# A two-layer decoder trunk: gate projections moved from three earlier chunks to the last attention, with their input kept in DRAM

## The chip, the cores and the metric

The kernel runs on one core of one Trainium2 chip. The metric is the device time of one execution in microseconds (us). The engines are PE (TensorE, matmuls and transposes; its weight loads are counted as PEld), DVE (VectorE), ACT (ScalarE), POOL (GpSimd) and SP (SyncE, which here only issues DMAs). ACT and POOL issue some DMAs as well. Each engine works through its own instructions in order.

## The reference

Two layers over 2048 positions of width 1024, in float32. Layer 0 is a gated short convolution; keys and values are then computed once; layer 1 is a stick-breaking attention of 8 heads of 64, with its own query and SiLU gate.

```python
def _short_conv_mixer(h, w_in, w_conv, w_out):
    b_gate, c_gate, xin, g = jnp.split(h @ w_in, 4, axis=-1)
    y = b_gate * _causal_depthwise_conv(c_gate * xin, w_conv)
    return (y * jax.nn.silu(g)) @ w_out
# attention, for one block of 128 queries and all keys before them:
    z = jnp.einsum("bhqd,bhkd->bhqk", qb, kf[:, :, :kl]) * scale
    log_one_minus = jnp.where(mask, jax.nn.log_sigmoid(-z), 0.0)
    rev = lax.cumsum(log_one_minus, axis=3, reverse=True)
    weights = jnp.exp(jnp.where(mask, z + rev, -jnp.inf))
    outs.append(jnp.einsum("bhqk,bhkd->bhqd", weights, vf[:, :, :kl]))
# the whole:
    x = x + _short_conv_mixer(_rmsnorm(x, norm_a), w_in_a, conv_a, w_out_a)
    k, v = jnp.split(_rmsnorm(x, norm_kv) @ w_kv, 2, axis=-1)
    q, g = jnp.split(_rmsnorm(x, norm_b) @ w_in_b, 2, axis=-1)
    o = attention(q, k, v)
    x = x + (o * jax.nn.silu(g)) @ w_out_b
    return _rmsnorm(x, norm_f)
```

The product of the factors 1 - sigmoid(z) over the keys between a key and its query is what the kernel computes as a running product, so that a weight is sigmoid(z) times that product.

## The kernel before

The positions run backwards and are cut into four chunks of 512 (c = 0 to 3). All activations are kept transposed, channels on the 128 partitions and the 512 positions of the chunk on the free axis. A matmul operand is split into a high and a low float32r part (`split`: ACT casts, DVE or POOL subtracts), and a product is made of three matmuls (high by high, high by low, low by high). A group of 8 input blocks is 24 matmuls of 128x128 by 128x512 (`mm3`); `LIN` is the planner's cost of one such group.

Per chunk the work is:

- `mixer_in`: for each of 8 channel blocks the four groups C, X, B, G and the convolution; the result goes to DRAM. Chunks 0 and 1 go together at the start, and there the weights are loaded raw, split once, and the split weights stored in DRAM (`split_w`; 32 for the mixer, 16 for the key/value and the query/gate weights in `fold_gains`, 8 for `w_out_a` in the first `proj_out`, 8 for `w_out_b` near the end). All later uses load the split form. A split weight lies in one of four buffers (tag `whl`), a raw one in one of two (`wraw`). The store is issued on SP's queue.
- `proj_out`: 8 groups, the residual, and the normalised input `xn` of the projections, split, in one of two large buffers (tag `act`, `kept[c]`).
- `proj_k`, `proj_q`, `proj_v`, `proj_g`: four groups each from `kept[c]`. The gate's result goes through a sigmoid (ACT, L441) and a product (DVE, L442) to `sg_d` in DRAM.
- `attention`: for each head and each chunk of keys up to its own, four blocks of 128 queries: `z` by two matmuls (L486, L487), the two sigmoids on ACT (L489 into `R`, L491 into `w`), on the diagonal chunk two masks on POOL (L495), the running product along the keys on DVE (L500), the product with `w` on DVE (L504). Then the weights are transposed (L512), split, and multiplied with the values (L521, L522). The last column of an `R` is the carry to the next chunk of keys; for that POOL copies it into the first column of the next `R` (L499), which the product at L504 reads. There are five `R` buffers.
- `gated`, `out_b`, `out_stat`, `out_norm`: the attention's result times the gate, the output projection, and the last norm. The last head and the output of the last chunk are handled by `out_b_last`.

The order across phases is written by `merge`: it draws from several generators in turn, always from the one whose spent share of its planned cost is smallest. `F0` to `F4` are the shares of a mixer or an attention that go into one phase before the rest goes into the next; `TP` is the planned cost of all projections of one chunk. Within this order, which acts as a priority, the framework's scheduler places the instructions on the engines by its own model of time. In the last phases the matmul groups of the fill are cut into sixes and tied to the attention's progress (`fine`, `anchors`). The fill of the last attention before is `proj_rest(3)`, then the output projections and norms of chunks 0, 1 and 2.

Of the kernel before, what the change touches and what calls it, by code (L numbers as in the profile page):

```python
# [23 lines left out]

F0, F1, F2, F3, F4 = 0.4, 0.5, 0.65, 0.4, 0.6
S2, S3, S4, S7 = 2.0, 0.5, 3.0, 2.0
# [19 lines left out]
def kernel(  # L46
# [48 lines left out]
    q_d = [[dram.tile([P, 2, CH], F32, name=f"q_d_{c}_{h}") for h in range(NH // 2)] for c in range(NCH)]  # L95
    v_d = [dram.tile([P, 4, NH, 2, 64], F32, name=f"v_d_{c}") for c in range(NCH)]
    sg_d = [[dram.tile([P, CH], F32, name=f"sg_d_{c}_{h}") for h in range(NH // 2)] for c in range(NCH)]
    og_d = [[dram.tile([P, CH], F32, name=f"og_d_{c}_{h}") for h in range(NH // 2)] for c in range(NCH)]
# [90 lines left out]
    def split_w(raw, key, nm, kt=KD, eng=nc.vector):  # L189

        wt = w_tile(nm, kt)
        split(wt[:, 0], wt[:, 1], raw, eng)
        split_d[key] = dram.tile([P, 2, kt, P], F32, name=f"sw_{nm}")
        nc.sync.dma_start(out=split_d[key], in_=wt.bitcast(F32))
        return wt
# [176 lines left out]
    def proj_out(c):  # L372
# [22 lines left out]
        for k in range(KD):  # L395
            t = x1[:, k, :]
            nc.vector.tensor_mul(t, t, pb)
            split(xn[:, 0, k, :], xn[:, 1, k, :], t, nc.gpsimd if k in XNL else nc.vector)
        kept[c] = xn
        yield YP[c] * 24 * MM  # L400
# [51 lines left out]
    def proj_rest(c):  # L452
        yield from proj_k(c, 1)
        yield from proj_q(c, 1)
        yield from proj_v(c, 1)
        yield from proj_v(c, 2)
        yield from proj_v(c, 3)
        for i in (2, 3):
            yield from proj_k(c, i)
            yield from proj_q(c, i)  # L460
        for i in range(4):
            yield from proj_g(c, i)


    def attention(c, h, ot):
# [8 lines left out]
        for kc in range(c, -1, -1):  # L474
# [7 lines left out]
            for qi in range(4):  # L482
# [9 lines left out]
                if diag:  # L492

                    for blk, fill in ((R[:, lo + 1:lo + 1 + P], 1.0), (w[:, lo:lo + P], 0.0)):
                        nc.gpsimd.affine_select(out=blk, in_=blk, pattern=[[1, P]], base=0, channel_multiplier=-1,  # L495
                                                compare_op=ALU.is_gt, fill=fill)
                    nc.gpsimd.memset(R[:, lo:lo + 1], 1.0)
                else:
                    nc.gpsimd.tensor_copy(R[:, 0:1], carry[qi])  # L499
                nc.vector.tensor_tensor_scan(out=R[:, lo + 1:CH + 1], data0=R[:, lo + 1:CH + 1],  # L500
                                             data1=ones[:, 0:1].to_broadcast([P, CH - lo]),
                                             initial=R[:, lo:lo + 1] if diag else carry[qi], op0=ALU.mult, op1=ALU.mult)
                carry[qi] = R[:, CH:CH + 1]
# [168 lines left out]
    def chain(*gens):  # L672
        for g in gens:
            yield from g
# [23 lines left out]
    LIN = 24 * MM  # L698
    TA, TF, TR, TO = 32 * LIN, 11 * LIN, 13 * LIN, 4 * LIN

# [6 lines left out]
    def heads(lo, hi, c):  # L707
        for hb in range(lo, hi):
# [5 lines left out]
            else:  # L714
                nc.sync.dma_start(out=og_d[c][hb], in_=ot)

    TP = TF + TR
    m01 = mixer_in((0, 1))
# [12 lines left out]
    lo, hi = range(0, NB), range(NB, KD)  # L731
    fill = chain(proj_rest(3), gated_in(0), out_b(0, range(KD)), out_stat(0), gated_in(1),
                 out_b(1, lo), out_norm(0), out_b(1, hi), gated_in(2), out_stat(1),
                 out_b(2, lo), out_norm(1), out_b(2, hi), out_stat(2))
    merge((fill, TR + 3 * TO), (heads(0, 3, 3), 0.75 * ta(3)))
    tail = chain(gated_in(3, range(3)), take(last, NB * 9 * MM), out_norm(2), until(last, -1.0))
# [29 lines left out]
```

## Time and profile before

| | us |
|---|---|
| median of 3 runs | 1909.28 (1908.41 to 1910.37) |
| profiled execution | 1907.57 |
| span of its trace | 1905.8 |
| PE busy | 1784.0 |
| DVE busy | 1264.6 |
| ACT busy | 769.7 |
| POOL busy | 436.2 |

The span is from the first to the last instruction of the trace; the profiled execution is 1.8 us longer. A row of the profile such as `L442 DVE TENSOR_TENSOR sgb<-sgb,pg ... x16 | 10.9, 684 | 49.9 <-ACT sgb L441 49.9` reads: line 442 of the kernel, on DVE, writes `sgb` from `sgb` and `pg`, 16 times; 10.9 us busy in all and 684 ns for one; 49.9 us of idle time of its engine before them, most of which the named instruction ended. A row of the table by stretches gives the stretch and its length, then for each engine the busy us and the number of instructions, then the granted clock of PE, the busy share of the DMA engines and GB/s. A row of the waits gives who waited for whom, us in total, times, longest us. A row of the chain of waits gives the start, the length and the piece of work. A row of DMA issues ends in the size of one and the median us from issue to landing.

### The profile page before, as it was taken

Reading aid. Unit: us, or ns where it says so; the run is one execution under the profiler, and the core shown is the slowest. Engines: PE = TensorE matmul, PEld = TensorE weight load, DVE = VectorE, ACT = ScalarE, POOL = GpSimd, SP = SyncE. Lnnn points to the kernel's source line nnn. Section 1 sums busy time; section 2 is a strip of 40 time slices with the busy share of each in tenths; the row PEclk is TensorE's granted clock in tenths of the full one; section 3 lists DMA queues with packets and bytes.
Section 4 is the critical chain, followed back from the end, with each engine's and each line's share of the span. In section 5 each row is a group of like instructions: output and inputs, shape, how many; then the busy total and the mean of one; then the engine's idle time right before and its main releaser. Section 6 shows DMA issues by size and latency. Waiting matters only on the chain.

```text
span 1905.8 us, 24702 instructions
## 1 busy us (share of the span) xinstructions
PE 1784.0 (94%) x8312; PEld 1449.4 (76%) x8312; DVE 1264.6 (66%) x1895; ACT 769.7 (40%) x1481; POOL 436.2 (23%) x822
## 2 busy tenths in 40 slices
PE   7899999999999999999999999999979999878785
PEld 5787777778888888888788888888857788656563
DVE  7644554574334264428888346788897999999996
ACT  6312222241123133314545233444555666565553
POOL 5000000000011021103123112222422224654641
PEclk9999999999999999999999999999999999999897
DMA  9648787798887779776767776655746665877751
GB/s 314 210 150 248 248 254 237 243 312 304 295 284 270 258 237 286 246 262 224 242 211 268 238 253 219 202 175 197 258 144 196 197 199 193 284 225 250 252 177 50
DMA packets 226702, 443.64 MB, mean 233 GB/s; under 512 B 16912, under 2 KB 131600, under 8 KB 199952
## 3 DMA queue, kind: packets, MB, share of 16 engines
q1 hardware_dynamic: 166496, 383.30, 60.0%
q10 hardware_dynamic: 59920, 58.74, 10.9%
q8 instruction: 66, 1.08, 0.2%
q14 instruction: 60, 0.49, 0.1%
q0 software_dynamic: 160, 0.02, 0.1%
HBM read 314.34 MB, written 127.66 MB: 232 GB/s over the span
## 4 chain that ended last, share of the span: by engine, by line
PE 69%; DVE 14%; DMA 9%; issue 4%; ACT 2%; POOL 1%; SPq 0%; ACTq 0%; POOLq 0%; DVEq 0%
PE pX L216 8%; PE po L216 7%; PE pG L216 7%; PE pC L216 7%; PE pB L216 6%; PE pg L216 5%; PE pk L216 5%; PE pq L216 5%; PE pv L216 4%; PE wt L512 4%; DVE R L500 4%; PE av L522 3%; DVE w L504 2%; PE av L521 2%; PE z L486 2%
## 5 line engine op out<-in xcount | busy, mean ns | idle before, releaser
L500 DVE TENSOR_TENSOR_SCAN R<-R,R,ones 128x512 f32<-128x512 f32 x192 | 256.6, 1339 | 11.4 <-ACT R L489 11.1
L489 ACT ACTIVATE R<-z 128x512 f32<-128x512 f32 (+1 forms) x320 | 174.2, 544 | 173.1 <-DVE R L500 78.4
L174 DVE TENSOR_TENSOR wtl<-wt,wth 128x512 fp32r<-128x512 f32 (+1 forms) x320 | 185.6, 600 | 67.2 <-ACT wth L173 66.3
L504 DVE TENSOR_TENSOR w<-w,R 128x512 f32<-128x512 f32 (+1 forms) x320 | 212.2, 671 | 21.3 <-POOL R L499 3.0
L173 ACT CAST wth<-wt 128x512 fp32r<-128x512 f32 (+1 forms) x320 | 160.3, 526 | 160.1 <-PE wt L512 137.4
L216 PE MATMUL pC<-h,whl_C 128*128 128x512 f32 x768 | 197.1, 405 | 14.4 <-ACT whl_C L173 8.3
L216 PE MATMUL pG<-h,whl_G 128*128 128x512 f32 x768 | 186.6, 393 | 9.9 <-ACT whl_G L173 9.9
L499 POOL COPY R<-R 128x1 f32<-128x1 f32 x192 | 112.3, 585 | 360.8 <-DVE R L500 293.3
L216 PE MATMUL pX<-h,whl_X 128*128 128x512 f32 x768 | 187.6, 393 | 6.0 <-ACT cs L320 3.9
L216 PE MATMUL po<-y,whl_o 128*128 128x512 f32 x768 | 187.8, 394 | 2.0 <-DVE x L389 1.3
L512 PE MATMUL wt<-ident,w 128*128 128x128 f32 x1088 | 177.8, 278 | 9.2 <-DVE w L504 5.1
L216 PEld LDWEIGHTS pC<-h,whl_C 128*128 128x128 f32 x768 | 148.2, 195 | 49.4 <-ACT whl_C L173 8.3
L216 PE MATMUL pB<-h,whl_B 128*128 128x512 f32 x768 | 185.6, 392 | 0.0
L216 PEld LDWEIGHTS pG<-h,whl_G 128*128 128x128 f32 x768 | 143.2, 188 | 41.0 <-ACT whl_G L173 11.6
L491 ACT ACTIVATE w<-z 128x512 f32<-128x512 f32 (+1 forms) x320 | 172.7, 543 | 0.5 <-PE wt L512 0.5
L216 PEld LDWEIGHTS pX<-h,whl_X 128*128 128x128 f32 x768 | 142.2, 188 | 37.6 <-ACT cs L320 5.1
L216 PEld LDWEIGHTS po<-y,whl_o 128*128 128x128 f32 x768 | 144.2, 189 | 33.5 <-DVE x L389 1.9
L512 PEld LDWEIGHTS wt<-ident,w 128*128 128x128 f32 x1088 | 138.6, 143 | 38.3 <-DVE w L504 7.2
L216 PEld LDWEIGHTS pB<-h,whl_B 128*128 128x128 f32 x768 | 143.0, 188 | 30.1 <-DVE cv L356 0.4
L522 PE MATMUL av<-wtl,vv 128*128 128x512 f32 (+1 forms) x320 | 129.1, 405 | 36.7 <-DVE wtl L174 36.6
L500 DVE TENSOR_TENSOR_SCAN R<-R,ones 128x512 f32<-128x512 f32 (+3 forms) x128 | 116.1, 913 | 33.8 <-POOL R L495 32.2
L486 PE MATMUL z<-kt,q 128*128 128x512 f32 (+1 forms) x320 | 129.1, 405 | 4.1 <-ACT w L491 3.4
(170 smaller groups left out, 2655.3 us busy)
## 6 DMA issues: line engine op xcount, KB each, us to landing
whl_o<-sw_o SPq DMA_DIRECT2D x24, 1024.0 KB, 5.7
kt<-k_d ACTq DMA_DIRECT2D x80, 256.0 KB, 3.6
vv<-v_d ACTq DMA_DIRECT2D x80, 256.0 KB, 4.0
whl_C<-sw_C SPq DMA_DIRECT2D x16, 1024.0 KB, 5.4
whl_X<-sw_X SPq DMA_DIRECT2D x16, 1024.0 KB, 5.5
whl_B<-sw_B SPq DMA_DIRECT2D x16, 1024.0 KB, 5.5
whl_G<-sw_G SPq DMA_DIRECT2D x16, 1024.0 KB, 5.2
whl_k<-sw_kv SPq DMA_DIRECT2D x16, 1024.0 KB, 5.2
```

The lines of the kernel that those rows point to most:

```text
L173: nc.scalar.copy(hi, src)
L174: eng.tensor_sub(lo, src, hi.bitcast(F32))
L216: ins = nc.tensor.matmul(ps, w[:, k, :], a[:, m, k, :], start=n == 0, stop=n == 3 * kt - 1)
L486: nc.tensor.matmul(ps[:, lom:CH], q2[:, 0, qi * P:(qi + 1) * P], kt[:, lom:CH], start=True, stop=False)
L489: nc.scalar.activation(R[:, lo + 1:CH + 1], ps[:, lo:CH], AF.Sigmoid, scale=-0.125)
L491: nc.scalar.activation(w[:, lo:CH], ps[:, lo:CH], AF.Sigmoid, scale=0.125)
L499: nc.gpsimd.tensor_copy(R[:, 0:1], carry[qi])
L500: nc.vector.tensor_tensor_scan(out=R[:, lo + 1:CH + 1], data0=R[:, lo + 1:CH + 1], data1=ones[:, 0:1].to_broadcast([P, CH - lo]), initial= ...
L504: nc.vector.tensor_mul(w[:, lo:CH], w[:, lo:CH], R[:, lo:CH])
L512: nc.tensor.transpose(wt[:, qi * P:(qi + 1) * P], ws[qi][:, kb * P:(kb + 1) * P], ident)
L521: nc.tensor.matmul(av[:, 0:n], vs, wh[:, 0:n], start=first, stop=False)
L522: ins = nc.tensor.matmul(av[:, 0:n], vs, wl[:, 0:n], start=False, stop=final)
```

## The change

The normalised, split input `xn` of chunks 0, 1 and 2 is also stored in DRAM, piece by piece, on POOL's queue. The four gate groups of these chunks leave `proj_rest` and become `proj_gate`, which reloads `xn` into a buffer of the tag `act` on SP's queue; in the fill of the last attention they stand behind those of chunk 3 and ahead of the output projections. The planned costs and four of the five shares are changed to go with it. Two further edits come along: the store of every split weight is issued on POOL's queue in place of SP's, and in the attention the carry is no longer copied into `R`: the first column of `R` is set to 1 by a POOL memset, and the running product starts at that column with the carry as its initial value.

```diff
-F0, F1, F2, F3, F4 = 0.4, 0.5, 0.65, 0.4, 0.6
+F0, F1, F2, F3, F4 = 0.3, 0.25, 0.6, 0.35, 0.6
...
+    xn_d = [dram.tile([P, 2, KD, CH], F32, name=f"xn_d_{c}") for c in range(NCH - 1)]
...
         split_d[key] = dram.tile([P, 2, kt, P], F32, name=f"sw_{nm}")
-        nc.sync.dma_start(out=split_d[key], in_=wt.bitcast(F32))
+        nc.gpsimd.dma_start(out=split_d[key], in_=wt.bitcast(F32))
...
             split(xn[:, 0, k, :], xn[:, 1, k, :], t, nc.gpsimd if k in XNL else nc.vector)
+            if c < NCH - 1:
+                nc.gpsimd.dma_start(out=xn_d[c][:, :, k, :], in_=xn[:, :, k, :].bitcast(F32))
...
             yield from proj_k(c, i)
             yield from proj_q(c, i)
+
+    def proj_gate(c, again=True):
+        if again:
+
+            kept[c] = act_tile(f"xa_{c}")
+            for k in range(KD):
+                nc.sync.dma_start(out=kept[c][:, :, k, :].bitcast(F32), in_=xn_d[c][:, :, k, :])
         for i in range(4):
             yield from proj_g(c, i)
...
-                    nc.gpsimd.memset(R[:, lo:lo + 1], 1.0)
-                else:
-                    nc.gpsimd.tensor_copy(R[:, 0:1], carry[qi])
-                nc.vector.tensor_tensor_scan(out=R[:, lo + 1:CH + 1], data0=R[:, lo + 1:CH + 1],
-                                             data1=ones[:, 0:1].to_broadcast([P, CH - lo]),
-                                             initial=R[:, lo:lo + 1] if diag else carry[qi], op0=ALU.mult, op1=ALU.mult)
+                nc.gpsimd.memset(R[:, lo:lo + 1], 1.0)
+                nc.vector.tensor_tensor_scan(out=R[:, lo:CH + 1], data0=R[:, lo:CH + 1],
+                                             data1=ones[:, 0:1].to_broadcast([P, CH + 1 - lo]),
+                                             initial=1.0 if diag else carry[qi], op0=ALU.mult, op1=ALU.mult)
...
-    TA, TF, TR, TO = 32 * LIN, 11 * LIN, 13 * LIN, 4 * LIN
+    TA, TF, TR, TG, TO = 32 * LIN, 11 * LIN, 13 * LIN, 4 * LIN, 4 * LIN
...
-    TP = TF + TR
+    TP = TF + TR - TG
...
-    fill = chain(proj_rest(3), gated_in(0), out_b(0, range(KD)), out_stat(0), gated_in(1),
+
+    fill = chain(proj_rest(3), proj_gate(3, False), proj_gate(0), proj_gate(1), gated_in(0), proj_gate(2),
+                 out_b(0, range(KD)), out_stat(0), gated_in(1),
                  out_b(1, lo), out_norm(0), out_b(1, hi), gated_in(2), out_stat(1),
                  out_b(2, lo), out_norm(1), out_b(2, hi), out_stat(2))
-    merge((fill, TR + 3 * TO), (heads(0, 3, 3), 0.75 * ta(3)))
+    merge((fill, TR + 3 * TG + 3 * TO), (heads(0, 3, 3), 0.75 * ta(3)))
```

## Prediction

> **What bounds the kernel now.** I read the page's busy shares and its forty slices first, to see whether one engine is the bound all the way.
>
> ```profile
> span 1905.8 us, 24702 instructions
> PE 1784.0 (94%) x8312; PEld 1449.4 (76%) x8312; DVE 1264.6 (66%) x1895; ACT 769.7 (40%) x1481; POOL 436.2 (23%) x822
> ...
> PE   7899999999999999999999999999979999878785
> ...
> DVE  7644554574334264428888346788897999999996
> ```
>
> PE (the matmuls) is at 9 from the second slice or so on, and falls to 8 and 7 only in the last eight slices, where DVE stands at 9. The 66% of DVE is a mean over a middle with room and an end without. So I cut the span at the places where the work changes: the first mixer (to 400), the dense middle, the pause ahead of the last chunk's projections (1400 to 1435), and the last attention with its fill, before and after its projections run out at 1600.
>
> ```profile
> core 0: us, PE busy (x) PEld busy (x) DVE busy (x) ACT busy (x) POOL busy (x), PEclk, DMA share, GB/s
> 0.00:50.00 50.00, 38.81 (x149) 28.60 (x150) 36.28 (x54) 29.93 (x47) 27.71 (x30) 1.00 1.02 315
> 50.00:400.00 350.00, 328.68 (x1425) 268.25 (x1424) 184.11 (x262) 87.53 (x113) 15.03 (x32) 0.98 0.72 227
> 400.00:450.00 50.00, 49.20 (x216) 40.06 (x215) 28.43 (x45) 15.63 (x22) 0.18 (x1) 1.00 1.04 373
> 450.00:1400.00 950.00, 946.64 (x4548) 787.29 (x4547) 559.50 (x873) 344.13 (x723) 183.10 (x448) 1.00 0.73 243
> 1400.00:1435.00 35.00, 23.84 (x109) 16.22 (x108) 34.74 (x68) 21.88 (x45) 10.04 (x25) 0.90 0.27 82
> 1435.00:1600.00 165.00, 158.53 (x810) 129.87 (x808) 145.73 (x195) 98.44 (x199) 46.47 (x92) 1.00 0.62 202
> 1600.00:1885.00 285.00, 234.26 (x1055) 176.26 (x1053) 265.42 (x374) 167.65 (x327) 149.35 (x191) 0.92 0.67 214
> ```
>
> From 450 to 1400 PE is busy 946.6 of 950 us: what is taken off PE there comes off the span. From 1600 to 1885 PE idles 50.7 us and DVE is busy 93%: attention's scans and products set the pace and PE waits for them, as the waits of that stretch say:
>
> ```profile
> PE av L522 <- DVE wtl L174: 26.5, 26, 3.6
> PE pob L216 <- DVE x1o L591: 4.7, 4, 2.1
> ```
>
> So the kernel has two bounds in turn, PE and then DVE, and work that needs much PE and little DVE is worth less time at the end than in the middle.
>
> **Part by part: the gates.** Twelve gate projections (four in each of the first three chunks) leave the middle and are put beside the last attention. The chain of waits shows what one costs where it lies now, and the groups what hangs on it:
>
> ```profile
> 581.14 5.44 PE pg L216 x24
> ...
> 598.42 5.50 PE pg L216 x24
> ```
>
> ```profile
> L442 DVE TENSOR_TENSOR sgb<-sgb,pg 128x512 f32<-128x512 f32 x16 | 10.9, 684 | 49.9 <-ACT sgb L441 49.9
> L441 ACT ACTIVATE sgb<-pg 128x512 f32<-128x512 f32 x16 | 9.6, 598 | 53.6 <-PE pg L216 53.5
> ```
>
> Twenty-four matmuls take 5.44 us, and they lie on the chain. 12 x 5.44 = **65.3 us** come off the middle. Its DVE load rises from 559.5 of 950 (59%) to (559.5 - 8.2) of 885 (62%), so DVE doesn't become the bound there.
>
> In the end, 1435 to 1885, PE is busy 158.5 + 234.3 = 392.8 of 450 us, which leaves room for 57.2; 65.3 are put in, so PE alone would need 8.1 us more. DVE is busy 145.7 + 265.4 = 411.2 of 450 (91.4%) and gets 12 x 0.684 = 8.2 us; at the same share that is 9.0 us more. Both say that the end grows by about **9 us**: it gets nearly full on both engines at once. ACT (266 of 450) takes 12 x 0.598 us without notice. That both can be nearly full together is seen from 1435 to 1600: PE 96%, DVE 88%. Bounds: 0, if DVE closes its own gaps with more PE work queued, and 33, priced as a rival.
>
> **Their input, kept in DRAM.** 24 pieces of 512 KB are stored and read back, and the gates' weights and results move along.
>
> ```profile
> whl_gg<-sw_b SPq DMA_DIRECT2D x16, 1024.0 KB, 5.4
> ...
> sg_d<-sgb SPq DMA_DIRECT2D x16, 256.0 KB, 4.8
> ...
> whl_ob<-sw_ob SPq DMA_DIRECT2D x16, 512.0 KB, 4.6
> ```
>
> At the end the DMAs move 165 x 202 + 285 x 214 = 94.3 MB now (KB/us times us). Added are 12 weights of 1.05 MB, 24 reads of 0.52 MB and 12 results of 0.26 MB: 28.3 MB. That makes 122.6 MB in 459 us, 267 GB/s, while 400 to 450 moves 373 GB/s with PE busy 49.2 of 50. A chunk's read is 4.2 MB, 11 us at that rate and 20 at 214 GB/s; its buffer (one of two) comes free when the gates of the chunk before the previous one are done, so four gates, 21.8 us of PE and as much again of attention between, cover it. If that cover is gone, PE, which works in order, waits up to 20 us in all. I take **+2** (0 to +20). In the middle the stored 12.6 MB replace weights of the same size: 0.
>
> **The scan.** A memset now takes the place of the copy of the carry, and the scan runs over one more element and waits for the memset, where earlier only the product behind it waited for the copy.
>
> ```profile
> L499 POOL COPY R<-R 128x1 f32<-128x1 f32 x192 | 112.3, 585 | 360.8 <-DVE R L500 293.3 <-DVE w L504 23.2 <-DVE t_x L138 10.9
> L497 POOL MEMSET R<- 128x1 f32 x128 | 11.4, 97 | 70.1 <-DVE R L500 56.7 <-DVE w L504 9.5 <-DVE h L246 2.5
> L500 DVE TENSOR_TENSOR_SCAN R<-R,ones 128x512 f32<-128x512 f32 x32 | 41.0, 1280 | 12.4 <-POOL R L495 12.3
> L500 DVE TENSOR_TENSOR_SCAN R<-R,ones 128x384 f32<-128x384 f32 x32 | 33.7, 1052 | 9.5 <-POOL R L495 9.0
> L610 POOL TENSOR_TENSOR x2r<-x2r,pbs 128x512 f32<-128x512 f32 x24 | 37.5, 1580 | 9.0 <-ACT pbs L605 6.0 <-ACT x2r L609 2.6 <-PE av L521 0.3
> DVE w L504 <- POOL R L499: 3.0, 1, 3.0
> ```
>
> One element more is (1280 - 1052) / 128 = 1.8 ns, 0.6 us over 320 scans. POOL saves 192 x (585 - 97) ns = 94 us, but isn't the bound; at the end DVE waited 3.0 us for the copy. What is new: a memset that is queued behind a 1.58 us POOL product delays the scan, and POOL is busy 149 of 285 us there. The last chunk has 96 such scans; the slack is the product that DVE does between (about 0.7 us). If one in four waits the mean remainder of a long operation beyond the slack, 0.4 us, that is 10 us, less the 3.0 gained and less what falls into stretches where PE is the bound. I take **+4** (-3 to +25).
>
> **Stores on POOL's queue.** All 64 stores of split weights leave SP's queue. On the chain of the first mixer it looks like this:
>
> ```profile
> 173.26 1.24 DVE whl_kv L174
> 174.51 5.01 DMA sw_kv<-whl_kv
> ...
> 179.62 1.05 ACT whl_G L173
> ...
> 180.72 1.22 PE pG L216 x2
> ...
> 361.97 5.01 DMA sw_b<-whl_b
> ```
>
> ```profile
> SPq L194 <- DVE whl_kv L174: 42.7, 8, 13.5
> ```
>
> The landing of a store frees one of four weight buffers, and PE waits for the split that goes into it; the chain holds five landings of this kind before 400, of which the first and the last stand here. Loads queued on SP behind a waiting store gain little: they need the raw buffer that the same subtraction frees, so the 0.32 us of an issue each. What POOL's landing costs is bounded by the only DMAs it issues now, and ACT's of the same kind:
>
> ```profile
> g_a<-in_norm_a_dram ACTq DMA_DIRECT2D x1, 4.0 KB, 4.6
> g_kv<-in_norm_kv_dram POOLq DMA_DIRECT2D x1, 4.0 KB, 7.0
> ...
> cw<-in_conv_a_dram POOLq DMA_DIRECT2D x1, 12.0 KB, 9.3
> POOL halo L335 <- DVE p L333: 300.3, 16, 23.0
> ```
>
> 2.4 to 4.7 us later, times five, is 12 to 23 us; these move 1024 and 3072 single elements, though, and a weight is 128 long rows, so I take 1 us each: **+5** (-4 to +23). The halo copies, which wait on POOL up to 23 us for their product, now share its queue with the stores; DVE does both what the stores and what the copies wait for, in one order, so I price that at 0 and keep it for a rival.
>
> The Trainium skill ("DMA: Bandwidth & Descriptors", Specifications) gives about 1 us to the first byte on the path of GpSimd's DMAs and 0.6 on that of SP and ACT. By it the five landings would cost 2 us in place of 5, an estimate from that page; the row of g_kv is larger than this, and no run yet shows a store of 1 MB.
>
> **New shares.** F0 and F1 leave more of the third chunk's mixer to run beside attention, as the middle now has fewer matmuls. With PE at 99.6% and DVE at 62% I take 0 (-6 to +10).
>
> **Sum**: -65.3 + 9 + 2 + 4 + 5 = -45.3. The profiled execution took 1907.6 (span 1905.8), so 1862.3; the median of the runs, 1909.3, is 1.7 above it: **1864.0**.
>
> **The rivals.** *The end gives half back.* PE's idle time at the end is in short waits (26 of 1 us, longest 3.6), and PE works in order: a gate's matmuls that sit ahead of a transpose hold DVE up, which has no slack. Then the end grows by 33 instead of 9: 1888. For it: DVE at 93% from 1600. Against: from 1435 to 1600 just such projections stand beside the same attention, with PE at 96%. *Everything fits.* The end grows by nothing, the other prices are 0, and the 11.2 idle us at 1400 to 1435 close: -76.5, 1833. Against: that pause is DVE-bound (34.7 of 35), and its shares are unchanged. *Slower: weight buffers wait for POOL.* 56 stores before 435, over four buffers, are 14 turns each; if every turn is on the path and a store lands d later, whether by descriptors or behind a halo copy, the first mixer grows by 14 d. At d = 4.7 it is 66 us in place of 5: 1925. It passes the time before from d = 3.6 on. Against: only five landings are on the chain, and between two uses of a buffer lie three groups of 5.44 us.
>
> **How the numbers follow.** Forecast 0.64, half back 0.19, everything fits 0.06, slower by the buffers 0.11. About 0.2% is what a measurement of this kernel can tell from no change. Half back, with the other costs at their upper ends, reaches the time before in 0.04. So faster 0.85, same 0.04, slower 0.11. The range of 8 in 10 runs from 1838, with the lower ends of the unknown costs, to 1898, with half back and part of POOL's upper ends.
>
> **What would show it.** Right: 24 matmuls of a gate still at about 5.5 us, now after 1435 less 65, in a stretch where PE is busy over 95%; DVE near 91% from there to the end; that stretch 455 to 475 us long; the middle 65 us shorter and its PE still at 99%; the first mixer over by 395 to 415. Half back: DVE below 88% in the end, and waits of DVE for ACT or PE in tens of us. POOL's cost: DVE scans waiting for POOL's memset, or the chain of the first mixer full of store landings beyond 6 us. I am wrong if the middle doesn't shrink, or if the first mixer or the end each grow by over 30.

## The result, and the profile after

| | before | after |
|---|---|---|
| median of 4 runs, us | 1909.67 | 1956.57 (1953.72 to 1959.83) |
| profiled execution, us | 1907.57 | 1955.66 |
| span of its trace, us | 1905.8 | 1954.0 |

The ratio is 1.0247 (95% interval 1.0229 to 1.0265): the changed kernel is 47 us slower. The forecast was 45 us faster, so the prediction was wrong, and in sign. First the changed kernel's page, its busy shares and slices:

```profile
span 1954.0 us, 24892 instructions
PE 1804.4 (92%) x8312; PEld 1465.3 (75%) x8312; DVE 1266.3 (65%) x1895; ACT 766.7 (39%) x1481; POOL 401.3 (21%) x910
...
PE   7899889989899999999999999999889999987794
...
DVE  7644444454434286386747458877878877899895
```

The same number of matmuls and DVE instructions takes 48 us more. PE's own busy time is 20 us higher (1804.4 against 1784.0). PE now has 8s among slices 5 to 11, where it had only 9s, and DVE falls from 9 to 7 or 8 in slices 30 and 32 to 35. Cut into stretches (same columns as before):

```profile
50.00:428.00 378.00, 343.33 (x1429) 277.50 (x1428) 184.01 (x263) 86.74 (x113) 39.13 (x76) 0.94 0.60 213
428.00:530.00 102.00, 88.34 (x380) 72.30 (x379) 50.24 (x93) 23.92 (x36) 13.84 (x23) 0.93 0.87 318
...
939.00:1400.00 461.00, 457.38 (x2228) 379.75 (x2227) 319.49 (x474) 194.19 (x402) 68.10 (x229) 1.00 0.69 231
...
1435.00:1680.00 245.00, 240.53 (x1193) 198.99 (x1192) 190.07 (x247) 121.96 (x248) 36.54 (x122) 0.99 0.74 252
1680.00:1933.00 253.00, 211.61 (x936) 161.97 (x934) 225.25 (x322) 143.44 (x278) 121.51 (x170) 0.90 0.72 232
```

For the comparison of kernels I use marks that each of them has: its first matmul of `po` (the first output projection) for chunks 0 and 3, and its first `pk` for chunks 0 and 3. From `pk` of chunk 3 to the end is called the last stretch. All are read from one trace each, and executions of one kernel differ by several us (those of `gates_old`, below, ran from 1897 to 1909), so a few us between two stretches mean nothing.

| us | `po` 0 | `pk` 0 | `po` 3 | `pk` 3 | end | last stretch |
|---|---|---|---|---|---|---|
| before | 400 | 491 | 1329 | 1431 | 1906 | 475 |
| after | 428 | 529 | 1330 | 1430 | 1954 | 524 |

The first mixer ends 28 us later. PE is busy 343.3 of 378 us to 428, where it was 328.7 of 350 to 400: 13 of the 28 us are longer idle time, and 15 are longer busy time for about as many matmuls (1429 and 1425), at a granted clock of 0.94 in place of 0.98. Another 10 us are lost by `pk` 0. By `pk` 3 all of that is made good, because the gates are out of the middle, where PE is full as before (457.4 of 461 from 939 to 1400). The last stretch is 49 us longer. In the rows, its part with projections has PE busy 240.5 of 245 us and DVE only 190.1 (78%); its second part still leaves PE 41.4 us idle.

### The profile page after: what moved, and what is told of

The parts are those of the page before. It is cut to its first block, busy times and chain, and to the rows that moved or that the text cites. A ratio compares the mean times of both kernels' runs of the same rounds, so it can differ in the third digit from the quotient of the medians.

```text
span 1954.0 us, 24892 instructions
## 1 busy us (share of the span) xinstructions
PE 1804.4 (92%) x8312; PEld 1465.3 (75%) x8312; DVE 1266.3 (65%) x1895; ACT 766.7 (39%) x1481; POOL 401.3 (21%) x910
## 4 chain that ended last, share of the span: by engine, by line
PE 60%; DVE 12%; DMA 11%; issue 4%; ACT 2%; POOL 1%; SPq 0%; ACTq 0%; POOLq 0%; DVEq 0%
PE po L217 8%; PE pC L217 6%; PE pX L217 6%; PE pG L217 5%; PE pB L217 5%; PE wt L520 4%; PE pg L217 4%; DVE R L508 4%; PE pv L217 3%; PE pk L217 3%; PE pq L217 3%; PE av L530 3%; PE av L529 2%; PE z L496 2%; PE z L497 2%
## 5 line engine op out<-in xcount | busy, mean ns | idle before, releaser
L508 DVE TENSOR_TENSOR_SCAN R<-R,R,ones 128x513 f32<-128x513 f32 x192 | 253.3, 1325 | 13.8 <-ACT R L499 9.7
L217 PE MATMUL pX<-h,whl_X 128*128 128x512 f32 x768 | 204.9, 419 | 26.4 <-DVE cv L357 19.2
L512 DVE TENSOR_TENSOR w<-w,R 128x512 f32<-128x512 f32 (+2 forms) x320 | 211.5, 669 | 16.3 <-POOL R L505 0.5
L217 PEld LDWEIGHTS pX<-h,whl_X 128*128 128x128 f32 x768 | 154.3, 203 | 65.4 <-issue 21.6
L529 PE MATMUL av<-wth,vv 128*128 128x512 f32 (+1 forms) x320 | 123.4, 386 | 13.7 <-ACT wth L174 10.3
L507 POOL MEMSET R<- 128x1 f32 x320 | 30.6, 104 | 456.9 <-DVE R L508 391.7
```

Of the source, the lines that this page charges most:

```text
L217: ins = nc.tensor.matmul(ps, w[:, k, :], a[:, m, k, :], start=n == 0, stop=n == 3 * kt - 1)
L508: nc.vector.tensor_tensor_scan(out=R[:, lo:CH + 1], data0=R[:, lo:CH + 1], data1=ones[:, 0:1].to_broadcast([P, CH + 1 - lo]), initial=1.0 ...
L512: nc.vector.tensor_mul(w[:, lo:CH], w[:, lo:CH], R[:, lo:CH])
L529: nc.tensor.matmul(av[:, 0:n], vs, wh[:, 0:n], start=first, stop=False)
```

## The experiments

Ratios are to the kernel before, measured beside each kernel on the same chip. In the diffs `-` and `+` are relative to the kernel named.

### Stores of split weights on POOL's queue

One kernel undoes this in the changed kernel, the other does this alone in the kernel before.

```diff
# stores_sp, from the changed kernel
-        nc.gpsimd.dma_start(out=split_d[key], in_=wt.bitcast(F32))
+        nc.sync.dma_start(out=split_d[key], in_=wt.bitcast(F32))
# before_stores_pool, from the kernel before: the reverse
```

> The changed kernel with one part undone: split weights are stored on SP's queue again. Theory 'landing': a store on POOL lands 7.3 us after its issue where SP's takes 5.0, it holds one of four weight buffers so much longer, and that is why the first output projection starts at 428 in place of 400 and why PE idles 13.7 us between 428 and 530. Then the first output projection starts at 400 (+-5) again, the idle of the following 100 us falls under 5, and the time falls by 35 to 42 to about 1918 us. Rival 'order': the first mixer is slower because the scheduler places its work differently, not because of the store itself; then it starts after 415 and the time stays above 1940. Theory 'place' (the gates lie where PE is already full, and the DVE-bound stretch behind them keeps its idle time): whatever happens before, the stretch from chunk 3's first key projection (1430) to the end stays at 520 to 530 us, where the kernel before takes 475.

> The kernel before with one part of the change alone: split weights are stored on POOL's queue. 'Landing': the first output projection starts at 425 to 432 in place of 400, and the time rises by 30 to 42, to 1940 to 1950 us. 'Order': by less than 12 us, under 1921.

Measured: 1923.16 (1.0081, 1.0066 to 1.0096) with the stores back on SP, so 32 us are regained; 1938.05 (1.0158, 1.0143 to 1.0173) with this edit alone, so 30 are lost. `po` 0 comes at 401 and 425. The edit costs about 30 us by itself, either way round. The DMA issues of the kernel before, then of the changed one (last number: median us from issue to landing):

```profile
sw_C<-whl_C SPq DMA_DIRECT2D x8, 1024.0 KB, 5.1
...
sw_X<-whl_X SPq DMA_DIRECT2D x8, 1024.0 KB, 5.8
sw_B<-whl_B SPq DMA_DIRECT2D x8, 1024.0 KB, 6.1
...
sw_kv<-whl_kv SPq DMA_DIRECT2D x8, 1024.0 KB, 5.0
sw_b<-whl_b SPq DMA_DIRECT2D x8, 1024.0 KB, 5.0
```

```profile
sw_C<-whl_C POOLq DMA_DIRECT2D x8, 1024.0 KB, 7.1
sw_X<-whl_X POOLq DMA_DIRECT2D x8, 1024.0 KB, 7.3
...
sw_B<-whl_B POOLq DMA_DIRECT2D x8, 1024.0 KB, 7.9
...
sw_kv<-whl_kv POOLq DMA_DIRECT2D x8, 1024.0 KB, 7.3
sw_b<-whl_b POOLq DMA_DIRECT2D x8, 1024.0 KB, 7.3
```

For the six weights of the first mixer a store of 1 MB lands 1.5 to 2.3 us later from POOL (`sw_G`, not shown: 5.0 and 7.0); for `sw_o`, most of which comes behind `po` 0, it is 8.0 and 8.2. Pieces of the changed kernel's chain of waits (start, length, work):

```profile
181.98 6.79 DMA sw_kv<-whl_kv
...
204.34 7.01 DMA sw_kv<-whl_kv
...
213.79 9.50 DMA wr_B<-in_w_in_a_dram
...
230.57 8.30 DMA wr_fold_kv<-in_w_kv_dram
```

Five landings of stores stand on it before 428, as there were five before 400, and together they are only 7.5 us longer (32.6 against 25.1). Raw loads make up more of it too: 67 us of the stretch from 160 to 400 in the kernel before, 77 from 160 to 428 here, and 100 from 160 to 425 in the kernel with this edit alone. The split and the convolution run late on DVE, and PE waits for that. The waits of PE from 50 to 400 in the changed kernel:

```profile
PE pX L217 <- DVE cv L357: 19.2, 6, 4.4
PE pC L217 <- DVE cv L346: 6.6, 5, 4.3
```

In the kernel before the same two were 2.1 and 4.3 us. The first goes back to 1.9 with the stores on SP and is 19.7 with this edit alone. The other part, the longer busy time, stands in groups such as the first of these two in the changed kernel, each of 24 matmuls:

```profile
330.60 8.49 PE pX L217 x24
339.09 5.46 PE pB L217 x24
```

The granted clock was 0.65 in the first and 1.00 in the second. With this edit alone the clock stayed at 0.98 and most of the loss, 19 of 24 us, is idle time of PE.

My reading was that the price is a delay in each turn of the four buffers, and not only in the turns that stood on the old chain. 14 turns of 1.5 to 2.3 us are 21 to 32, and 28 were measured at `po` 0. That agreement is loose: only 50 stores, 12.5 turns, were issued by then, and half of the 28 us are longer busy time of PE. Nor do the waits ended by a store's landing grow by as much: 19.2 us from 50 to 400 before, 18.4 here to 428, 27.5 to 425 with this edit alone. One rival the traces rule out: that the stores hold up the halo copies on POOL. DVE waited 0.9 us for those, in the changed kernel as with this edit alone.

The rival 'order' stays. Its time limits were missed, but up to `po` 0 DVE runs the same 315 instructions in exactly two orders: one in the two kernels with the stores on SP, another in the two with the stores on POOL. So the edit is shown as the cause of the 30 us; how much of it is late landings and how much the other order was not separated.

### The scan

```diff
# scan_old, from the changed kernel; before_scan_new is the reverse in the kernel before
-                nc.gpsimd.memset(R[:, lo:lo + 1], 1.0)
...
+                    nc.gpsimd.memset(R[:, lo:lo + 1], 1.0)
+                else:
+                    nc.gpsimd.tensor_copy(R[:, 0:1], carry[qi])
...
+                                             initial=R[:, lo:lo + 1] if diag else carry[qi], op0=ALU.mult, op1=ALU.mult)
```

> The changed kernel with the running product as before: POOL copies the carry, the scan starts one column later. Rival 'memset' (scans wait for a POOL memset queued behind long POOL work): DVE's waits for POOL before its scans vanish and the time falls by 15 to 25, to 1932 to 1942 us. Theories 'landing' and 'place' give this edit less than 5 us either way: 1952 to 1961.

> The kernel before with the new running product alone (memset in place of the copy, one element more). From the pair with and without it in the changed kernel: 0 to 7 us slower, 1908 to 1915. 'Memset' as first priced: 1912 (+4). A gain of over 4 us would speak for POOL's 94 us less of copies having held something up.

Measured: 1951.82 (1.0235, 1.0218 to 1.0251) with the old scan, 1912.30 (1.0022, 1.0009 to 1.0035) for the new scan alone. The edit costs 4 us (2 to 7), as forecast. DVE's waits for POOL ahead of its scans, in the whole changed kernel and then in the kernel before:

```profile
DVE R L508 <- POOL R L505: 18.0, 19, 2.9
...
DVE R L508 <- POOL R L507: 2.9, 3, 1.9
```

```profile
DVE R L500 <- POOL R L495: 32.2, 26, 5.2
```

The memset itself (L507) is hardly waited for: 2.9 us here, 1.3 with this edit alone. The other waits are for POOL's masks (L505, before L495), on the diagonal chunk, and they were there before (30.9 us with this edit alone). So the 4 us don't lie in waits for POOL. This edit too changes the order of DVE's instructions, from the 423rd of 1895 on in the kernel before; where the 4 us lie is not shown.

### The shares

```diff
# shares_old, from the changed kernel
-F0, F1, F2, F3, F4 = 0.3, 0.25, 0.6, 0.35, 0.6
+F0, F1, F2, F3, F4 = 0.4, 0.5, 0.65, 0.4, 0.6
```

> The changed kernel with the five shares of the kernel before. Rival 'shares' (smaller shares of the third chunk's mixer leave projections without cover in the middle, 428 to 939): the middle from the first output projection to that of chunk 3 (902 us now) shrinks by 20 to 30, to 1927 to 1937 us in all. 'Landing' and 'place': the middle changes by less than 8 us and the time stays within 1948 to 1965.

Measured: 1943.74 (1.0198, 1.0175 to 1.0221). By the ratios the new shares cost 9 us (some 4 to 15), not 0. Neither expectation fits whole: from `po` 0 to `po` 3 the kernel is 22 us shorter with the old shares, as 'shares' had it, but the time falls by less. The first stretch from `po` 0 on and the sum over all up to `pk` 3, in the changed kernel and then with the old shares:

```profile
428.00:529.00 101.00, 87.34 (x375) 71.50 (x374) 49.56 (x92) 23.92 (x36) 13.84 (x23) 0.93 0.87 317
...
sum 1002.00, PE 963.60 PEld 794.42 DVE 614.72 ACT 375.94 POOL 164.80; mean PE 192.72 PEld 158.88 DVE 122.94 ACT 75.19 POOL 32.96
```

```profile
427.00:534.00 107.00, 102.84 (x443) 84.18 (x443) 51.65 (x95) 25.58 (x38) 13.92 (x22) 0.97 0.85 303
...
sum 985.00, PE 959.33 PEld 792.82 DVE 611.69 ACT 373.59 POOL 164.16; mean PE 191.87 PEld 158.56 DVE 122.34 ACT 74.72 POOL 32.83
```

From `po` 0 to `pk` 3 PE idles 38.4 us with the new shares and 25.7 with the old ones. Most of the difference lies in the first stretch (13.7 against 4.2), where the first projections run and a smaller F0 puts less of the third chunk's mixer beside them. Why PE then runs dry, and whether it would with the stores on SP, was not tried.

### The gates alone, and what of them is their input

`gates_old` is the move of the gates and nothing else: old shares, old scan, all stores on SP, those of `xn` too. `gates_xnpool` puts the stores of `xn` on POOL. `no_reload` leaves the 24 stores and 24 reads out, and the moved gates read chunk 3's input.

```diff
# gates_xnpool, from gates_old
-                nc.sync.dma_start(out=xn_d[c][:, :, k, :], in_=xn[:, :, k, :].bitcast(F32))
+                nc.gpsimd.dma_start(out=xn_d[c][:, :, k, :], in_=xn[:, :, k, :].bitcast(F32))
# no_reload, from gates_old
-            if c < NCH - 1:
-                nc.sync.dma_start(out=xn_d[c][:, :, k, :], in_=xn[:, :, k, :].bitcast(F32))
...
-            kept[c] = act_tile(f"xa_{c}")
...
+            kept[c] = kept[3]
```

> The move of the gates alone: all stores on SP, the running product and the five shares as in the kernel before. If the parts add up (stores 33, shares 13, scan 0 to 5 us), the time is 1900 to 1912 us. Theory 'place' (gates lie where PE is full already): the middle is 60 to 66 us shorter than before, and the stretch from chunk 3's first key projection to the end 520 to 530 us where the kernel before takes 475.

> The gates alone, with the 24 stores of the inputs on POOL's queue, as in the change, in place of SP's. Leaving stores and reloads out gained 12.8 us, 10 of them ahead of chunk 3's first key projection. If it is SP's order that costs these 10 (loads queued behind stores that wait for a split): 1896 to 1901 us, first key projection of chunk 3 at 1374 to 1379. If it is the transfers themselves: 1903 to 1910.

> The gates alone, but the gates of chunks 0 to 2 read chunk 3's input, which lies in SBUF: the 24 stores and 24 reads of the inputs are left out. 'Reload': the stretch from chunk 3's first key projection to the end falls by 15 to 40 us. 'Place': by less than 8.

| | us | ratio (95%) | `po` 3 | `pk` 3 | end | last stretch |
|---|---|---|---|---|---|---|
| before | | 1 | 1329 | 1431 | 1906 | 475 |
| gates_old | 1906.33 | 0.9977 (0.9961 to 0.9993) | 1276 | 1384 | 1900 | 517 |
| gates_xnpool | 1907.66 | 0.9994 (0.9983 to 1.0006) | 1277 | 1385 | 1908 | 523 |
| no_reload | 1893.62 | 0.9911 (0.9886 to 0.9936) | 1268 | 1374 | 1895 | 520 |

The move alone makes the kernel 4 us faster (1 to 7). It does bring 47 us by `pk` 3, where 60 to 66 were expected, and the last stretch takes 42 of them back. The stores of `xn` cost the middle about 10 us (`pk` 3 at 1374 without them), on either queue: that points to the stores themselves, not to SP's order. Leaving the reads out, and with them the buffer that they fill, brings nothing in the last stretch. So what are the 42 us? First where they show, the last stretch of `gates_old`:

```profile
1384.00:1500.00 116.00, 112.68 (x559) 92.51 (x558) 88.75 (x120) 57.84 (x119) 29.55 (x56) 0.99 0.67 220
1500.00:1637.00 137.00, 133.81 (x658) 110.73 (x657) 107.87 (x137) 70.02 (x141) 42.83 (x69) 0.99 0.78 272
...
1700.00:1750.00 50.00, 42.35 (x188) 32.04 (x187) 46.92 (x65) 31.76 (x60) 30.08 (x34) 0.90 0.80 262
1750.00:1800.00 50.00, 40.99 (x180) 31.73 (x181) 48.30 (x75) 30.56 (x60) 27.33 (x39) 0.88 0.74 236
```

Until 1637 PE is 97 to 98% busy and DVE 77 to 79%; from 1700 PE is at 82 to 85% and DVE at 94 to 97%. The gates came into the first part, where PE had no room. The idle time of PE that the forecast counted on lies in the second part, beside the output projections, and most of it is still there (34.7 us from 1637 to 1879). The last chunk's attention falls behind early: its third head ends 218 us after `pk` 3 where it ended at 189, so 29 of the 42 us are lost by then. The waits of DVE in the last stretch, before and in `gates_old`:

```profile
DVE wtl L174 <- ACT wth L173: 11.9, 12, 4.0
```

```profile
DVE wtl L175 <- ACT wth L174: 42.9, 33, 8.0
```

ACT rounds the transposed weights for DVE and gets them late. That PE's transposes are late behind the gates' matmuls was my reading of it; it is tried next.

### Taking the suspects away, one and all

Four kernels, each with the cuts of the one before it as well. In `light_gates` each moved gate does 3 of its 24 matmuls. In `light_noreload` `xn` is neither stored nor read back, as in `no_reload`. In `empty_gates` a moved gate loads an eighth of its weight. In `empty_zero` the planner gives it no cost.

```diff
# light_gates, from gates_old
-        yield from mm3(ps, wts, kept[c])
+        kt = KD if c == NCH - 1 else 1
+        yield from mm3(ps, wts, kept[c], kt=kt)
...
-        yield rest(24)
+        yield rest(24) if c == NCH - 1 else 24 * MM
# empty_zero, from empty_gates
-        yield rest(24) if c == NCH - 1 else 24 * MM
+        yield rest(24) if c == NCH - 1 else 0.0
...
-    merge((fill, TR + 3 * TG + 3 * TO), (heads(0, 3, 3), 0.75 * ta(3)))
+    merge((fill, TR + 3 * TO), (heads(0, 3, 3), 0.75 * ta(3)))
```

> The gates alone (old stores, scan and shares), but each of the twelve moved gates does 3 of its 24 matmuls; seven eighths of its contraction are left out, while its weights, its reloaded input, its sigmoid, product and store stay. 57 us of PE are gone from the last stretch, and nothing else. Theory 'place' in its first half (the gates lie where PE is the bound, so their PE time counts there in full): the stretch from chunk 3's first key projection to the end falls from 516 by 33 to 50 us, to what the kernel before takes (475), and the time to 1856 to 1873. Rival 'hand-overs' (the growth is from the gates' DMAs, ACT and DVE work): it stays above 500.

> The moved gates with 3 of 24 matmuls each (as in the run with light gates), and now also without the stores and reloads of their inputs; what is left out is seven eighths of their contraction and the right inputs for chunks 0 to 2. Theory 'either is enough' (beside the last attention the gates' PE time and the traffic of their reloads each fill the same time, so that taking one away alone gains nothing): the last stretch falls well below the 516 to 525 us of the runs that lack only one of them, to 480 to 500. Rival 'order' (the stretch is long because of how the fill and attention are ordered and handed over, whatever the gates do): 505 or more.

> The same, and the moved gates load only the eighth of their weights that they use: of the moved work are left 36 matmuls, twelve sigmoids, products and stores. 'Either is enough', or weights as the rest of the traffic: 474 to 488 us for the last stretch, and a time of 1850 to 1870. 'Order': 505 or more, time over 1885.

> The empty gates (3 of 24 matmuls, an eighth of the weights, no reloads), now with a planned cost of 0, so that attention stands to the rest of the fill as in the kernel before. Theory 'plan' (the 23 us by which the last stretch of the empty gates still exceeds the 475 of the kernel before come from the planned cost of the gates: the fill ahead of them is drawn faster and the heads fall behind): the last stretch falls from 500 to 472 to 484 us, and the first three heads end 45 to 50 us apart with head 2 at 185 to 197 us after chunk 3's first key projection. Rival 'left-overs' (the twelve sigmoids, products and stores, and the buffers they take): 494 or more.

| | matmuls | `xn` | weights | planned | us | ratio (95%) | last stretch |
|---|---|---|---|---|---|---|---|
| gates_old | yes | yes | yes | yes | 1906.33 | 0.9977 | 517 |
| light_gates | few | yes | yes | yes | 1911.72 | 1.0028 (1.0015 to 1.0041) | 526 |
| no_reload | yes | no | yes | yes | 1893.62 | 0.9911 | 520 |
| light_noreload | few | no | yes | yes | 1874.36 | 0.9830 (0.9795 to 0.9865) | 497 |
| empty_gates | few | no | few | yes | 1873.61 | 0.9823 (0.9787 to 0.9859) | 500 |
| empty_zero | few | no | few | no | 1863.34 | 0.9772 (0.9749 to 0.9796) | 484 |

This refuted my theory, that the gates' PE time alone fills the part where PE is full: without it the last stretch isn't shorter. Without the reads alone it isn't either. Without both it is 20 us shorter; by the ratios `light_noreload` gains 15 us on `no_reload` alone. The stretch in question in `light_gates`, then in `no_reload`, and the waits of DVE in the last stretch of `light_gates`:

```profile
1500.00:1637.00 137.00, 100.86 (x428) 77.06 (x426) 103.93 (x134) 68.88 (x140) 39.17 (x63) 0.84 0.81 281
```

```profile
1500.00:1637.00 137.00, 135.75 (x678) 112.54 (x677) 108.19 (x144) 71.91 (x147) 44.25 (x77) 1.00 0.66 216
```

```profile
DVE wtl L175 <- ACT wth L174: 28.8, 21, 4.0
DVE R L511 <- ACT R L500: 14.2, 8, 4.8
```

With the reads gone, PE is still full: 135.8 of 137 us. With the matmuls gone, PE idles 36 us, DVE is no busier than with the full gates (76% against 79%), and the DMAs move 281 GB/s at a share of 0.81. Part of what holds the attention there is seen on ACT, which issues the attention's loads of keys, values and queries. Its waits that a landing ended, in `light_gates` from 1500 to 1637:

```profile
ACT R L500 <- DMA sga<-sg_d: 6.9, 1, 6.9
...
ACT wth L174 <- DMA xa<-xn_d: 5.6, 1, 5.6
...
ACT R L500 <- DMA sg_d<-sgb: 4.9, 1, 4.9
```

Each of these waits ends with ACT issuing a load of the attention (`kt` or `vv`), after a transfer of the fill, `xn` or a gate's result, has landed. They are 17 us together, and a fourth, behind a `vv`, is 3.2. In `gates_old` from 1480 to 1640 there are two, 9.7 and 3.3 us; in `no_reload` one of 1.1; in the kernel before and in `light_noreload` none. Why such a load waits for those landings is not shown. The matmuls that are left also run slower: over the whole last stretch `light_gates` has 252 matmuls fewer than `gates_old`, yet PE's busy time falls by 34 us and not by 57, at a granted clock of 0.88 in place of 0.93.

With matmuls and reads both gone, the attention moves. `empty_gates` in the stretch from 1500 on:

```profile
1500.00:1600.00 100.00, 77.39 (x352) 57.51 (x351) 92.19 (x120) 62.17 (x127) 32.76 (x61) 0.91 0.59 178
1600.00:1849.00 249.00, 208.69 (x933) 159.90 (x932) 227.88 (x328) 143.42 (x279) 135.41 (x167) 0.92 0.72 231
```

DVE is at 92% there, with PE and DMA both idle a good part of the time. The weights matter little (497 and 500; the 500 lies between the two expectations). The planned cost does: while a chunk's gates that do almost nothing still count as four groups, the planner thins out the attention beside them, and with that gone another 16 us go (10 by the medians), and the third head ends 189 us after `pk` 3, as in the kernel before. So of the 42 us some 17 to 20 need PE time and reads both away (either alone is enough to cost them), 10 to 16 are the order that the planner writes, and about 9 are left for the remaining matmuls, sigmoids, products and stores, and for the scatter of single traces. The planner's part was measured with emptied gates only; that it is as large with full gates is not shown.

### Spreading the gates, and speeding up what follows

If the gates' place is the fault, they could stand among the output projections, where DVE is the bound; and if the planner's order is, the output projections could be given less cost, so that the attention gets on with fewer of them beside it.

```diff
# spread_old, from gates_old; spread_noreload the same from no_reload
-    fill = chain(proj_rest(3), proj_gate(3, False), proj_gate(0), proj_gate(1), gated_in(0), proj_gate(2),
-                 out_b(0, range(KD)), out_stat(0), gated_in(1),
-                 out_b(1, lo), out_norm(0), out_b(1, hi), gated_in(2), out_stat(1),
+    fill = chain(proj_rest(3), proj_gate(3, False), proj_gate(0), gated_in(0), out_b(0, lo), proj_gate(1),
+                 out_b(0, hi), out_stat(0), gated_in(1),
+                 out_b(1, lo), out_norm(0), proj_gate(2), out_b(1, hi), gated_in(2), out_stat(1),
# pace_old, from gates_old: cost of the output projections and norms times FO = 0.43; pace_07: 0.7
+    def scaled(g, f):
+        for r in g:
+            yield r * f
...
-    merge((fill, TR + 3 * TG + 3 * TO), (heads(0, 3, 3), 0.75 * ta(3)))
+    merge((fill, TR + 3 * TG + 3 * FO * TO), (heads(0, 3, 3), 0.75 * ta(3)))
# paired, from gates_old: one load of a gate's weight serves two chunks, 3 with 0 and, behind out_b(0), 1 with 2
```

> The same with the gates of chunks 1 and 2 put between the output projections of chunks 0 and 1. 'Place': they now fall into the DVE-bound stretch with its idle PE, and the stretch from chunk 3's first key projection to the end falls by 20 to 35, to 490 to 505 us; time 1870 to 1885. Rival 'reload' (the end is long because 25 MB more go through the DMAs there): within 8 us of the run with the gates alone.

> The gates of chunks 1 and 2 between the output projections of chunks 0 and 1, but without the reload that held up the loads of the output projections there: they read chunk 3's input, as in the run without the reload, with which it is to be compared (last stretch 521 us, 1893.6). Theory 'place' in its second half (the idle PE time of the DVE-bound stretch can be filled with gates): the last stretch falls to 485 to 503. Rival 'own pace' (the output projections have a chain of their own, so that the stretch from the first of them to the end doesn't shrink when attention is taken from it, nor take more PE work): 512 or more.

> The gates as in the change, in the same order of the fill, but the planned cost of the output projections and norms of chunks 0 to 2 is scaled by 0.43, so that five of the six heads, not four, run beside projections and gates and one beside the output projections. 'Place': PE stays over 97% busy up to the last gate, DVE there rises from 78% to over 88%, and the last stretch falls to 485 to 505 us; time 1865 to 1885. 'Reload': within 8 us of the run with the gates alone.

> The full computation, gates moved alone, with the planned cost of the output projections scaled by 0.7. With 1 the last stretch is 516 us and the heads end 486 us after its start, 30 before the end; with 0.43 it is 528, and the heads end at 462, 66 before the end, with output projections left over. If a better balance lies between, 500 to 512 us and a time of 1890 to 1902; if 'either is enough' sets the length whatever the pace, 512 to 524, 1902 to 1914.

> The full computation, gates moved, stores, scan and shares as in the kernel before; but each load of gate weights serves two chunks (3 with 0, then 1 with 2), which takes 8.4 MB of loads out of the last stretch, and the second pair stands behind the output projection of chunk 0, which covers its reloads. 'Either is enough': the last stretch stays within 10 us of 516, since PE's share is all there; time 1896 to 1912. If traffic alone decides: 495 to 505, time 1885 to 1895.

| | us | ratio (95%) | last stretch |
|---|---|---|---|
| spread_old | 1926.34 | 1.0070 (1.0042 to 1.0099) | 548 |
| spread_noreload | 1904.95 | 0.9984 (0.9968 to 1.0000) | 530 |
| pace_old | 1912.62 | 1.0015 (1.0000 to 1.0029) | 528 |
| pace_07 | 1905.40 | 0.9982 (0.9965 to 0.9998) | 522 |
| paired | 1924.44 | 1.0087 (1.0054 to 1.0119) | 539 |

None does clearly better than `gates_old`. `spread_old` misses both of its expectations, and so does `paired`, whose longer stretch stays unexplained. `spread_noreload` speaks for 'own pace', and `pace_07` for 'either is enough'. Spread out, the reads of `xn` hold up the output projection's own loads, which follow them on SP's queue; the chain of `spread_old`:

```profile
1658.95 9.34 DMA xa<-xn_d
...
1668.31 6.92 DMA x<-x_d
```

Each of these starts when the one before it has landed. Without the reads the spread order is still 10 us longer in the last stretch than the order of `no_reload`, so the DVE-bound part doesn't take PE work for nothing either. With cheaper output projections (`pace_old`) the attention does get done sooner (its last head ends 462 us after `pk` 3, 487 before that edit), but then they are left over. `pace_old` from the end of the attention but for its last pieces:

```profile
1844.00:1889.00 45.00, 29.54 (x103) 20.91 (x103) 18.93 (x43) 12.96 (x20) 15.13 (x13) 0.81 0.59 190
```

For 45 us PE is busy 29.5 and DVE 18.9: work that had been hidden beside the attention now stands alone.

## Why the prediction was wrong

**The sum, measured.** By the ratios: the gates alone -4 us (forecast -65.3 + 9 + 2 = -54), the stores of split weights +30 to 32 (+5), the scan +2 to 4 (+4), the shares +9 (0), the stores of `xn` on POOL in place of SP some +3 (0; the interval of the difference touches 0). That makes 40 to 44 of the 47 us; what is missing lies within the intervals.

**What bounds the kernel, and the gates off the middle: right, but for a cost.** PE was the bound of the middle, and matmuls taken off it came off the time: `po` 3 came 53 us earlier with the gates alone, 61 with their input's stores gone, of 65.3 forecast. The step "the stored 12.6 MB replace weights of the same size: 0" was wrong: about 10 us. In the changed kernel `po` 0 to `pk` 3 is only 29 us shorter than before (1002 for 1031): some 17 go with the new shares, some 10 with the stores of `xn`, and some 9 of the 65.3 aren't accounted for.

**The gates into the end: the step that failed.** It read "PE is busy 158.5 + 234.3 = 392.8 of 450 us, which leaves room for 57.2; 65.3 are put in, so PE alone would need 8.1 us more". The step added up two stretches that it had itself shown to have different bounds. Of the 57.2 us, 50.7 lay after 1600, and the gates were put ahead of that, where PE was at 96%. The row quoted for it (PE 96%, DVE 88% from 1435 to 1600) showed that both can be nearly full; it showed as well that nothing more goes in there. The measured growth is 42 us for the gates alone and 49 in the changed kernel, in place of 11. The rival that the end gives half back named the right signs (DVE below 88%: 415 of 498 us, 83%; waits of DVE for ACT in tens of us) and priced them at 33. But its mechanism, a gate's matmuls ahead of a transpose, was only one of the causes: with those matmuls gone the stretch stayed as long (526 us). The reads and the planner's order were two more. The reads were sized by whether "four gates, 21.8 us of PE and as much again of attention between, cover it", that is by what they do to the gates; that ACT's loads for the attention would wait while such transfers land (13 us in `gates_old`, 17 in `light_gates`) was in no term.

**The stores on POOL: a second term far too small.** The forecast counted five landings on the chain at 1 us each, +5; measured 28 at `po` 0 and 30 to 32 in the time. A store lands 1.5 to 2.3 us later, so five of them are 7.5 us (32.6 against 25.1 on the chain), and the remaining 20 and more lie elsewhere: in raw loads on the chain, in matmuls at a lower granted clock, and in an order of DVE's work that changed with the edit. The step that failed is to price the edit by the landings on the old chain alone. The rival's form, 14 d, gives 21 to 32 with the measured d; its stated price used d = 4.7, from small transfers, and that each turn counts is not shown, so that its form comes near 28 may be luck. The Trainium skill ("DMA: Bandwidth & Descriptors", Specifications) gives about 1 us to the first byte on GpSimd's path and 0.6 on SP's, 0.4 us apart. The stores here landed 1.5 to 2.3 us later, so the measurement decides against the estimate of 2 us for five landings.

**The scan: the right number, by luck.** +4 was forecast and 2 to 4 measured. But the forecast put it down to scans that wait for the memset, one in four of 96, and these waits are 1.3 us with the edit alone and 2.9 in the changed kernel. **The shares: wrong**, 0 forecast and 9 measured, at the upper end of the stated bounds. The argument was that PE was at 99.6% in the middle; but other shares make another order, and that kept PE less full: 38.4 us idle from `po` 0 to `pk` 3 in place of 25.7.

**The range** missed since both large misses have the same sign. Half back and the buffers' rival were weighed as alternatives, and the chances never asked what both together would give: with 14 turns of 2.1 us, 29, it is 1864 + 33 - 9 + 29 - 5 = 1912, still without the shares and the planner's order.

No version with the whole computation is clearly better than the kernel before: `gates_old` and `pace_07` gain about 4 us. The last 9 us of the end, why ACT's loads wait for the landings of other transfers, the way in which the stores on POOL cost 30 us, and the detail of the shares stay open.

## What to carry to other kernels

Room on an engine is only room in the stretch where the work will stand: take the idle time of that stretch alone, and expect nothing from idle time that comes later. Where a buffer is held until a store has landed, the landings on the present chain are not the whole price of a slower store: here they grew by 7.5 us and the kernel by 30. An edit can also change the order that a scheduler writes, so compare the orders before you call the edited instruction itself the cause. When one suspected cost is taken away and nothing moves, take away two before you acquit it: here matmuls and reads were each enough by themselves. And when a forecast term comes out right, look whether the waits it was made of are there.

## What the runs showed of the hardware

The same stores of 1 MB landed 1.5 to 2.3 us later from POOL's queue than from SP's in the first mixer. Twenty-four matmuls of 128x128 by 128x512 took 5.46 us where the granted clock was 1.00 and 8.49 us where it was 0.65. The one-column memset on POOL took 104 ns on average where the copy of one column had taken 585, and that gave the kernel nothing:

```profile
L507 POOL MEMSET R<- 128x1 f32 x320 | 30.6, 104 | 456.9 <-DVE R L508 391.7
```
